# Three of a streaming kernel's loads split in two halves, one from each of two issuing queues

## The chip, the cores and the metric

The kernel runs on one core of a Trainium2 chip. A core has engines that run side by side: here ScalarE (ACT) takes exponentials (busy 124.1 us of a span of 162.2 us in the kernel before), VectorE (DVE) adds up rows (72.9 us), and SyncE (SP) issues the loads; ScalarE issues the final store, and after the change some loads too. The bytes themselves are moved by 16 DMA engines that both issuers share. A load is issued when an engine puts it on its queue. It has landed when its semaphore (a counter) has been raised for the last time: the traces show 16 raises for each load. Load 4, for instance, brings chunk 4 of the input. The metric is the device time of one execution in microseconds, lower is better. Each kernel was run several times, always in rounds beside the kernel before on the same chip.

## The reference

```python
# x: 32 x 512 x 1024, float32
x_max = np.max(x, axis=-1, keepdims=True)
return x_max.squeeze(-1) + np.log(np.sum(np.exp(x - x_max), axis=-1))
```

That is 16,384 rows of 1,024 numbers, 67.1 MB in, 64 KB out. The values come from a normal distribution, so the kernel leaves the maximum out and computes `log(sum(exp(x)))`.

## The kernel before

Each of the 128 partitions holds 128 rows of the input. They are loaded in 17 chunks into a ring of 51 row slots. A "row" below means one row for each of the 128 partitions, 512 KB.

```python
CHUNKS = [          # (rows, rows whose sum VectorE takes)
    (4, 1), (15, 11), (16, 10), (16, 15), (16, 0), (14, 0), (12, 9), (9, 5), (7, 5), (5, 4),
    (4, 3), (3, 0), (2, 2), (2, 2), (1, 0), (1, 0), (1, 0),
]
RING_ROWS = 51
...
    def load(i):
        (s, row), r = place[i], CHUNKS[i][0]
        act_wait = max(a for a, _ in busy[s : s + r])
        dve_wait = max(d for _, d in busy[s : s + r])
        if dve_wait:
            nc.sync.wait_ge(dve_done, dve_wait)
        if act_wait:
            nc.sync.wait_ge(act_done, act_wait)
        for engine, lo, hi in FIRST_PARTS if i == 0 else [("sync", 0, P)]:
            getattr(nc, engine).dma_start(
                out=ring[lo:hi, s : s + r], in_=x_v[lo:hi, row : row + r]
            ).then_inc(landed[i], 16)
...
    for i, (r, n_dve) in enumerate(CHUNKS):
        if i:
            load(i)
        ...
        nc.scalar.wait_ge(landed[i], 16 * (len(FIRST_PARTS) if i == 0 else 1))
        if n_dve:
            nc.scalar.activation(                       # one exponential over n_dve rows
                out=ring[:, s : s + n_dve], in_=ring[:, s : s + n_dve], func=Exp
            ).then_inc(act_done, 1)
            ...
            nc.vector.reduce_sum(out=sums[:, row : row + n_dve], ...)
        for j in range(n_dve, r):                       # the other rows: ScalarE sums as well
            nc.scalar.activation(..., func=Exp, accum_out=sums[:, row + j : row + j + 1])
    ...
    # take the logarithms, store the result from ScalarE
```

Chunks 0 to 3 fill the ring (4 + 15 + 16 + 16 = 51 rows), so loads 0 to 3 wait for nothing. Load 4 writes over slots of chunks 0 and 1 and waits for chunk 1's sums on VectorE; load 5 waits for those of chunk 2, loads 6 and 7 for those of chunk 3. All loads go out on SyncE's queue, the first as the first instruction of the program.

The softmax here doesn't subtract the row's maximum and nothing guards it: scores larger than these inputs give would overflow.

Of the kernel before, what the change touches and what calls it, by code (L numbers as in the profile page):

```python
# [1 line left out]

# [4 lines left out]



CHUNKS = [  # L10
# [4 lines that stand above are left out]

LN_AT = 5

FIRST_PARTS = [("sync", 0, 128)]


@with_exitstack
def kernel(
    ctx: ExitStack,
    tc: tile.TileContext,
    x: bass.AP,
    axis: bass.AP,
    out: bass.AP,
):
    nc = tc.nc
    P = nc.NUM_PARTITIONS  # L30

    assert axis in (-1, len(x.shape) - 1), f"only last-axis reduction supported, got {axis}"

    x_flat = x.flatten_outer_dims()
    N, D = x_flat.shape
    assert N % P == 0
    NB = N // P
    assert sum(r for r, _ in CHUNKS) == NB

    fp32 = mybir.dt.float32  # L40
    Exp = mybir.ActivationFunctionType.Exp
    Ln = mybir.ActivationFunctionType.Ln
    AX = mybir.AxisListType.X

    x_v = x_flat.rearrange("(p t) d -> p t d", p=P)
    out_v = bass.AP(tensor=out.tensor, offset=out.offset, ap=[[NB, P], [1, NB]])

    ring = nc.alloc_sbuf_tensor("ring", [P, RING_ROWS, D], fp32).ap()
    sums = nc.alloc_sbuf_tensor("sums", [P, NB], fp32).ap()
    res = nc.alloc_sbuf_tensor("res", [P, NB], fp32).ap()  # L50

    landed = [tc.alloc_semaphore(f"landed{i}") for i in range(len(CHUNKS))]
    act_done = tc.alloc_semaphore("act_done")
    dve_done = tc.alloc_semaphore("dve_done")
    stored = tc.alloc_semaphore("stored")


    hook = nc.pop_inst_callback()
    symbolic, nc._always_lower_symbolic_ap = nc._always_lower_symbolic_ap, False


    place = []
    row = slot = 0
    for r, _ in CHUNKS:
        if slot + r > RING_ROWS:
            slot = 0
        place.append((slot, row))
        slot += r
        row += r



    busy = [(0, 0)] * RING_ROWS
    acts = dves = 0
# [6 lines that stand above are left out]
            nc.sync.wait_ge(dve_done, dve_wait)  # L81
        if act_wait:
            nc.sync.wait_ge(act_done, act_wait)
        for engine, lo, hi in FIRST_PARTS if i == 0 else [("sync", 0, P)]:
            getattr(nc, engine).dma_start(
                out=ring[lo:hi, s : s + r], in_=x_v[lo:hi, row : row + r]
            ).then_inc(landed[i], 16)

    def take_logs(lo, hi, dve_wait, act_wait):
        nonlocal acts  # L90
        nc.scalar.wait_ge(act_done, act_wait)
        nc.scalar.wait_ge(dve_done, dve_wait)
        nc.scalar.activation(out=res[:, lo:hi], in_=sums[:, lo:hi], func=Ln).then_inc(  # L93
            act_done, 1
        )
        acts += 1

    body = nc.main_func.blocks[-1]
    assert not body.instructions
    load(0)  # L100
    n_early = len(body.instructions)

    nc.scalar.preload_act_table_set("natural_log_exp_and_others")  # L103

    logged = 0
    done_before = [(0, 0)]
    for i, (r, n_dve) in enumerate(CHUNKS):
        if i:
            load(i)
        s, row = place[i]  # L110
        if i == LN_AT:
            logged = row
            take_logs(0, logged, *done_before[i])
        nc.scalar.wait_ge(landed[i], 16 * (len(FIRST_PARTS) if i == 0 else 1))
        if n_dve:
            nc.scalar.activation(  # L116
                out=ring[:, s : s + n_dve], in_=ring[:, s : s + n_dve], func=Exp
            ).then_inc(act_done, 1)
            acts += 1
            nc.vector.wait_ge(act_done, acts)  # L120
            nc.vector.reduce_sum(  # L121
                out=sums[:, row : row + n_dve], in_=ring[:, s : s + n_dve], axis=AX
            ).then_inc(dve_done, 1)
            dves += 1
            for j in range(n_dve):
                busy[s + j] = (0, dves)
        for j in range(n_dve, r):
            nc.scalar.activation(  # L128
                out=ring[:, s + j],
                in_=ring[:, s + j],  # L130
                func=Exp,
                accum_out=sums[:, row + j : row + j + 1],
            ).then_inc(act_done, 1)
            acts += 1
            busy[s + j] = (acts, 0)
        done_before.append((dves, acts))

    take_logs(logged, NB, dves, acts)
    nc.scalar.wait_ge(act_done, acts)
    nc.scalar.dma_start(out=out_v, in_=res).then_inc(stored, 16)  # L140
    nc.gpsimd.wait_ge(stored, 16)



    first = nc.main_func.blocks[0]
    head, work = first.instructions, body.instructions
    end = next(k for k, i in enumerate(head) if i.opcode == "UnconditionalBranch")
    head, tail = head[:end], head[end:]
    for ins in work[:n_early]:
        at = next(  # L150
            k for k, i in enumerate(head) if i.engine == ins.engine and i.opcode == "Drain"
        )
        head.insert(at, ins)
    first.instructions = head + work[n_early:] + tail
    body.instructions = []

    nc._always_lower_symbolic_ap = symbolic
    nc.push_inst_callback(hook)


# [1 line left out]
_INS = ['x', 'axis']  # L162
_OUTS = [((32, 512), 'float32')]

_NUMBERS = {'axis': -1}


# [26 lines left out]
```

## Time and profile before

| | before |
|---|---|
| time, median of the first 3 runs | 164.13 us (164.01 to 164.53) |
| span of the profiled run | 162.2 us |
| ACT busy, DVE busy | 124.1 us, 72.9 us |
| bytes read, mean rate | 67.11 MB, 414 GB/s over the span |
| last load landed | 158.08 us |

The first view is the table of stretches: for each stretch of time its length, then the busy time of DVE, ACT and POOL, the clock granted to TensorE (not used here), the mean busy share of the 16 DMA engines, and the GB/s. In brackets is the number of instructions. The stretches are cut at the moments when a chunk's work starts.

```profile
0.00:7.40 7.40, 0.00 (x0) 1.28 (x1) 0.20 (x4) 1.00 1.02 416
7.40:25.60 18.20, 1.22 (x1) 4.17 (x7) 0.00 (x0) 1.00 1.01 436
25.60:45.00 19.40, 9.76 (x1) 13.77 (x10) 0.00 (x0) 1.00 1.00 432
45.00:64.30 19.30, 12.68 (x2) 14.95 (x13) 0.00 (x0) 1.00 1.00 435
64.30:83.70 19.40, 6.57 (x2) 14.05 (x4) 0.00 (x0) 1.00 0.98 426
83.70:100.60 16.90, 9.85 (x1) 16.87 (x33) 0.00 (x0) 1.00 0.99 427
100.60:158.10 57.50, 32.03 (x7) 57.50 (x68) 0.00 (x0) 1.00 0.97 415
158.10:162.20 4.10, 0.77 (x1) 1.48 (x5) 0.00 (x0) 1.00 0.06 16
```

Read the second figure from the right, the DMA share: it is 0.97 to 1.02 in every stretch up to 158.1 us. From the first packet, at 1.08 us, the engines that move the bytes are practically never idle: the trace's own packet records show 16 packets in flight at nearly every moment (exactly 16 in 94% of the moments from 2.5 to 157 us, 16.05 on average), as many as there are engines. Shares a little over 1 arise because a packet is booked whole to the stretch in which it starts. Then read ACT: in the first five stretches it has idle time (14.05 of 19.40 us busy before 83.7), from 83.7 us on it has none (57.50 of 57.50).

The second view is the timeline, here only the lines with which each chunk starts on ACT: start, duration, instruction, and in brackets how long ACT had been idle and what ended it.

```profile
7.42 1.06 ACT L116 ACTIVATE ring<-ring 128x1024 f32<-128x1024 f32 x1 [5.37 <-DMA ring<-in_x_dram]
25.62 9.59 ACT L116 ACTIVATE ring<-ring 128x11264 f32<-128x11264 f32 x1 [14.02 <-DMA ring<-in_x_dram]
44.98 8.74 ACT L116 ACTIVATE ring<-ring 128x10240 f32<-128x10240 f32 x1 [5.62 <-DMA ring<-in_x_dram]
64.36 13.00 ACT L116 ACTIVATE ring<-ring 128x15360 f32<-128x15360 f32 x1 [4.42 <-DMA ring<-in_x_dram]
83.69 1.06 ACT L128 ACTIVATE ring<-ring 128x1024 f32<-128x1024 f32 x1 [5.29 <-DMA ring<-in_x_dram]
```

Each of the first five chunks starts when its load lands. The spacing of 19.4 us between chunks of 16 rows is 1.21 us a row, which is what the DMA engines need: the packet records show one packet for each partition's piece of a load, 65,536 bytes in 2.42 us, and 16 engines at that pace make 433 GB/s.

The trace's issue records tell the third thing: SyncE issued loads 0 to 3 at 0.00, 0.78, 1.16 and 1.95 us, each taking 0.33 to 0.74 us. Load 0 is not through until about 7 us. So issue time was hidden before the change.

### The profile page before, as it was taken

How to read it: one execution, taken by the hardware profiler on the slowest of the kernel's cores; microseconds unless marked ns; L12 is line 12 of the kernel's file. 1: busy time of each engine (PE TensorE's matmuls, PEld its weight loads, DVE VectorE, ACT ScalarE, POOL GpSimd, SP SyncE). 2: the span in 40 equal slices, each digit the busy share in tenths (PEclk: the TensorE clock that was granted, in tenths of full speed). 3: DMA queues.
4: the chain of work that ended last, by engine and by line, in shares of the span. 5: the costliest groups of instructions: out<-in, count | busy, mean ns of one | idle time of the engine just before them, and what ended most of it. 6: DMA issues, size and time to landing. Idle time of an engine off the chain costs nothing.

```text
span 162.2 us, 213 instructions
## 1 busy us (share of the span) xinstructions
DVE 72.9 (45%) x11; ACT 124.1 (76%) x136; POOL 0.2 (0%) x4
## 2 busy tenths in 40 slices
DVE  0030000039960799000999900000006999799591
ACT  3180006997099971999339999999999999999993
POOL 0000000000000000000000000000000000000000
DMA  6999899969969959969988999999999999999970
GB/s 263 497 485 470 349 394 517 485 291 517 485 291 517 517 259 517 517 275 501 517 368 370 424 424 432 461 497 388 436 427 399 431 400 439 420 424 414 415 318 16
DMA packets 2593, 67.18 MB, mean 414 GB/s; under 512 B 288, under 2 KB 416, under 8 KB 800
## 3 DMA queue, kind: packets, MB, share of 16 engines
q1 hardware_dynamic: 2448, 67.11, 96.4%
q10 hardware_dynamic: 144, 0.07, 0.1%
q14 instruction: 1, 0.01, 0.0%
HBM read 67.11 MB, written 0.07 MB: 414 GB/s over the span
## 4 chain that ended last, share of the span: by engine, by line
ACT 52%; DMA 38%; DVE 7%; issue 1%
DMA ring<-in_x_dram 38%; ACT ring L128 30%; ACT ring L116 22%; DVE sums L121 7%; ACT res L93 0%
## 5 line engine op out<-in xcount | busy, mean ns | idle before, releaser
L121 DVE TENSOR_REDUCE sums<-ring 128x5 f32<-128x5120 f32 (+8 forms) x11 | 72.9, 6648 | 86.0 <-ACT ring L116 85.9
L116 ACT ACTIVATE ring<-ring 128x5120 f32<-128x5120 f32 (+8 forms) x11 | 59.3, 5394 | 29.4 <-DMA ring<-in_x_dram 29.4
L128 ACT ACTIVATE ring<-ring 128x1024 f32<-128x1024 f32 x61 | 63.4, 1041 | 5.3 <-DMA ring<-in_x_dram 5.3
L128 ACT ACTIVATION_READ_ACCUMULATOR ring<-ring 128x1 f32 x61 | 11.4, 187 | 0.0
L103 ACT ACT_TABLE_LOAD x1 | 1.3, 1283 | 0.8 <-PEq L175 0.8
L93 ACT ACTIVATE res<-sums 128x67 f32<-128x67 f32 (+1 forms) x2 | 0.5, 256 | 0.1
L175 POOL MEMSET const-bfloat16-1.0<- 128x1 bf16 x1 | 0.1, 101 | 0.0
L175 POOL MEMSET const-uint8-127<- 128x1 uint8 x1 | 0.1, 101 | 0.0
L175 POOL MEMSET const-float32-0.0<- 128x1 f32 x1 | 0.1, 98 | 0.2 <-issue 0.2
L175 POOL MEMSET const-float32-1.0<- 128x1 f32 x1 | 0.1, 98 | 0.0
## 6 DMA issues: line engine op xcount, KB each, us to landing
ring<-in_x_dram SPq DMA_DIRECT2D x1, 7680.0 KB, 24.8
ring<-in_x_dram SPq DMA_DIRECT2D x1, 7168.0 KB, 36.1
ring<-in_x_dram SPq DMA_DIRECT2D x1, 6144.0 KB, 21.6
ring<-in_x_dram SPq DMA_DIRECT2D x1, 4608.0 KB, 32.1
ring<-in_x_dram SPq DMA_DIRECT2D x2, 2048.0 KB, 26.3
ring<-in_x_dram SPq DMA_DIRECT2D x1, 3584.0 KB, 40.2
ring<-in_x_dram SPq DMA_DIRECT2D x1, 2560.0 KB, 44.4
ring<-in_x_dram SPq DMA_DIRECT2D x2, 1024.0 KB, 46.0
```

Source lines behind the costliest of these rows:

```text
L93: nc.scalar.activation(out=res[:, lo:hi], in_=sums[:, lo:hi], func=Ln).then_inc(act_done, 1)
L103: nc.scalar.preload_act_table_set("natural_log_exp_and_others")
L116: nc.scalar.activation(out=ring[:, s : s + n_dve], in_=ring[:, s : s + n_dve], func=Exp).then_inc(act_done, 1)
L121: nc.vector.reduce_sum(out=sums[:, row : row + n_dve], in_=ring[:, s : s + n_dve], axis=AX).then_inc(dve_done, 1)
L128: nc.scalar.activation(out=ring[:, s + j], in_=ring[:, s + j], func=Exp, accum_out=sums[:, row + j : row + j + 1],).then_inc(act_done, 1)
L175: nc = _bacc.Bacc("TRN2", target_bir_lowering=False, num_devices=1)
```

## The change

The intent is to put the first big loads on two issuing queues at once: loads 1, 2 and 3 are cut in two halves by rows, the first half issued by SyncE, the second by ScalarE, which is idle then (for 5.37 us before its first exponential). ScalarE's three issues stand after its table load and before its first exponential.

```diff
-FIRST_PARTS = [("sync", 0, 128)]
+SHARED = (1, 2, 3)
...
-        for engine, lo, hi in FIRST_PARTS if i == 0 else [("sync", 0, P)]:
-            getattr(nc, engine).dma_start(
-                out=ring[lo:hi, s : s + r], in_=x_v[lo:hi, row : row + r]
+        half = r // 2 if i in SHARED else r
+        nc.sync.dma_start(
+            out=ring[:, s : s + half], in_=x_v[:, row : row + half]
+        ).then_inc(landed[i], 16)
+        if half < r:
+            nc.scalar.dma_start(
+                out=ring[:, s + half : s + r], in_=x_v[:, row + half : row + r]
             ).then_inc(landed[i], 16)
...
+    for i in SHARED:
+        load(i)
...
-        if i:
+        if i and i not in SHARED:
             load(i)
...
-        nc.scalar.wait_ge(landed[i], 16 * (len(FIRST_PARTS) if i == 0 else 1))
+        nc.scalar.wait_ge(landed[i], 32 if i in SHARED else 16)
```

## The prediction

> **What bounds it now.** The table of stretches shows a DMA share of 0.97 to 1.02 in every stretch from 0 to 158.1 us (415 to 436 GB/s), against 0.06 in the last 4.1 us. Queue q1 alone takes 96.4% of 16 engines' span. In the trace's packet records 16 packets are in flight at nearly every moment: each row of 65,536 B takes 2.42 us, one of 61,440 B 2.27 us, one of 16,384 B 0.61 us, the next starting as one ends. The load stream is the floor: about 67.1 MB at 430 GB/s, plus 1.1 us before the first packet, about 1.2 us of slow first packets (0.95 to 1.36 us instead of 0.61), and 4 us of tail. ACT is the second bound: it waits for landings before 83.7 us (at 7.4, 25.6, 45.0, 64.4, 83.7), then is busy 57.50 of 57.50 us to the end, each chunk ending just as the next lands.
>
> **What the change does.** The same bytes, in 20 loads instead of 17. Removed: nothing on the DMA engines; SyncE had issued its first four loads by 2.4 us, 4 us before the first of them ended, so issue time was hidden already. Added: 24 more packets per engine. From 0.611 us for 16 KB and 2.42 us for 64 KB the fixed part of a packet is about 8 ns, so about 0.2 us in all. Three issues on ACT (0.3 to 0.75 us each, as on SyncE) fall into ACT's idle 5.37 us before its first exponential: free.
>
> **What moves.** [...] No part of this trace has two load queues at once, so the order below is an estimate. ACT's halves arrive at about 2 us, while load 0 still has some six packets per engine to go; these will alternate with 32 KB packets (1.2 us): load 0 lands at about 13 instead of 7.4. When SyncE's half of load 1 is through, ACT's queue is already most of the way through load 2's half: 25 rows have gone instead of 19, at 1.21 us a row: load 1 lands at about 33 (25.6 before), load 2 at about 52 (45.0), load 3 unchanged at 64.4.
>
> **Critical path.** Following the durations: chunk 1's sums end at 54 (47.1 before), so load 4 is issued at 54, still before the queue runs dry at 64. Chunk 2's sums end at 72, load 5 is issued then, before 82. ACT does chunk 2 until 67, chunk 3 until 81, before load 4 lands at 83.7; loads 6 and 7 go out at about 96.4 (93.6 before), before load 5's last packets at 98 to 100. All of the delay is absorbed, with about 2 us left at the tightest places. From 83.7 us on everything is as before, later by 0.2 us.
>
> **Prediction.** 164.3 us, 163.7 to 165.4. Chances: faster by over 2% 0.02, within 2% 0.92, slower by over 2% 0.06.
>
> **What would show it.** Landings of loads 0, 1, 2 later by 6 to 7 us, of loads 3 and 4 unchanged; DMA share still 1.0 from 1 to 158 us; ACT's first wait about 11 us instead of 5.4; ACT without idle after 84.
>
> **What would make it wrong.** A cost of switching between queues[...]. A landing order worse than estimated, so that ACT still has work at 83.7 or load 6 comes after the queue has run dry: each microsecond over then adds one. Faster only if two queues raise the engines' rate, or the slow first packets shrink.

The forecast's sum came to 164.1 us of the kernel before and 0.2 us for 24 more packets an engine, 164.3 us. That the two queues alternate by packet was the assumption at that point, and the landings in "What moves" are an estimate that rests on it; the packet records below show the alternation.

## The result

The changed kernel took 164.37 us (median of 4 runs, 164.19 to 164.70), the kernel before in the same comparison 164.09. The ratio is 1.0013, with a 95% interval of 0.9994 to 1.0033: the same. Ratios here and below are the mean time of one kernel's fast runs over that of the other's of the same rounds, so not quite the ratio of the medians.

The table of stretches of the changed kernel, with the same cuts:

```profile
0.00:7.40 7.40, 0.00 (x0) 1.28 (x1) 0.20 (x4) 1.00 0.90 354
7.40:25.60 18.20, 1.22 (x1) 4.17 (x7) 0.00 (x0) 1.00 1.01 434
25.60:45.00 19.40, 4.81 (x1) 13.74 (x9) 0.00 (x0) 1.00 1.00 431
45.00:64.30 19.30, 12.61 (x2) 14.30 (x12) 0.00 (x0) 1.00 1.07 462
64.30:83.70 19.40, 11.10 (x2) 14.60 (x5) 0.00 (x0) 1.00 0.98 426
83.70:100.60 16.90, 10.35 (x1) 16.64 (x32) 0.00 (x0) 1.00 0.99 427
100.60:158.10 57.50, 31.80 (x7) 57.47 (x68) 0.00 (x0) 1.00 0.97 415
```

The DMA share is full again, and the rates are the same. (The 0.90 of the first stretch and the 1.07 of the fourth come from packets booked whole to the stretch in which they start; the records show the engines taking one packet after the other in both.) The queues' lines of the page, packets, MB, and share of 16 engines' span, show where the halves went: q1 is SyncE's queue, q10 ScalarE's.

```profile
q1 hardware_dynamic: 2448, 54.53, 78.6%
q10 hardware_dynamic: 576, 12.65, 18.1%
```

Together 96.7%; before, q1 alone had 96.4%. And the starts of the chunks on ACT, from the timeline:

```profile
12.34 1.06 ACT L122 ACTIVATE ring<-ring 128x1024 f32<-128x1024 f32 x1 [10.28 <-DMA ring<-in_x_dram]
30.57 9.59 ACT L122 ACTIVATE ring<-ring 128x11264 f32<-128x11264 f32 x1 [14.05 <-DMA ring<-in_x_dram]
50.00 8.74 ACT L122 ACTIVATE ring<-ring 128x10240 f32<-128x10240 f32 x1 [5.68 <-DMA ring<-in_x_dram]
64.87 12.99 ACT L122 ACTIVATE ring<-ring 128x15360 f32<-128x15360 f32 x1
83.96 1.06 ACT L134 ACTIVATE ring<-ring 128x1024 f32<-128x1024 f32 x1 [5.06 <-DMA ring<-in_x_dram]
```

Chunks 0, 1 and 2 start 4.9 to 5.0 us later than before. Chunk 3 starts 0.5 us later and needs no wait at all (no bracket), and chunk 4 starts 0.27 us later. So the change moved three landings by 5 us, and nothing of that is left at 84 us. Two questions follow: why did they move, and why did it cost nothing?

### The profile page after: what moved, and what is told of

It reads as the page before. It is cut to its first block, busy times and chain, and to the rows that moved or that the text cites. A ratio compares the mean times of both kernels' runs of the same rounds, so it can differ in the third digit from the quotient of the medians.

```text
span 162.4 us, 216 instructions
## 1 busy us (share of the span) xinstructions
DVE 72.9 (45%) x11; ACT 123.9 (76%) x136; POOL 0.2 (0%) x4
## 4 chain that ended last, share of the span: by engine, by line
ACT 52%; DMA 38%; DVE 7%; issue 1%
DMA ring<-in_x_dram 38%; ACT ring L134 30%; ACT ring L122 22%; DVE sums L127 7%; ACT res L97 0%; ACT L107 0%
```

## The experiments

The table collects the landing of each load (when the last part of its semaphore count arrived), ScalarE's first issue and the first packet on ScalarE's queue (on the earliest of the 16 engines), all from the traces' records, in us from the span's start, and the times.

| kernel | first issue, first packet | load 0 | 1 | 2 | 3 | 4 | last | median time | ratio (95%) |
|---|---|---|---|---|---|---|---|---|---|
| before | none | 7.4 | 25.6 | 45.0 | 64.3 | 83.7 | 158.1 | 164.1 | 1 |
| the change | 0.81, 4.60 | 12.3 | 30.6 | 50.0 | 64.6 | 83.9 | 158.3 | 164.37 | 1.0013 (0.9994 to 1.0033) |
| e1 halves, one queue | none | 7.6 | 25.8 | 45.2 | 64.7 | 84.0 | 158.8 | 164.46 | 1.0024 (1.0011 to 1.0038) |
| e2 load 1 only | 0.80, 4.56 | 12.2 | 25.8 | 45.1 | 64.7 | 84.1 | 158.6 | 164.41 | 1.0013 (0.9996 to 1.0031) |
| e3 ACT after load 0 | 7.50, 11.34 | 7.5 | 30.5 | 50.1 | 74.3 | 84.0 | 164.0 | 169.71 | 1.0341 (1.0325 to 1.0356) |
| e4 ACT order 2, 1, 3 | 0.81, 4.54 | 12.3 | 40.3 | 50.0 | 64.5 | 85.7 | 160.1 | 166.03 | 1.0122 (1.0092 to 1.0152) |
| e5 ACT order 3, 1, 2 | 0.80, 4.66 | 12.4 | 40.6 | 60.0 | 64.8 | 85.8 | 164.4 | 170.19 | 1.0349 (1.0330 to 1.0367) |
| e6 ACT order 3, 2, 1 | 0.81, 4.54 | 12.3 | 59.6 | 49.9 | 64.5 | 103.4 | 179.1 | 185.28 | 1.1272 (1.1249 to 1.1294) |
| e7 half of load 4 | none | 7.5 | 25.9 | 45.3 | 64.6 | 74.3 | 154.1 | 160.02 | 0.9732 (0.9716 to 0.9748) |
| e8 half of load 5 | none | 7.6 | 25.7 | 45.1 | 64.4 | 83.8 | 153.9 | 164.02 | 0.9979 (0.9959 to 0.9999) |
| e9 load 0 in two parts | 1.28, 4.98 | 14.3 | 32.6 | 52.0 | 64.5 | 83.8 | 158.4 | one look, 164.33 | |
| e10 table after issue | 0.78, 4.79 | 12.3 | 30.5 | 50.0 | 64.5 | 83.9 | 158.7 | one look, 164.61 | |
| e11 ACT half first | 0.12, 2.81 | 16.2 | 34.4 | 54.0 | 64.9 | 84.2 | 160.2 | 166.20 | 1.0109 (1.0073 to 1.0145) |

My theory: (a) the DMA engines carry bytes at the same rate whoever issues them (432.5 GB/s from 2.5 to 64 us before, 431.6 with the change, from the packet records), so two queues can only change the order in which bytes land; (b) with two queues each engine takes packets from them in turn, so parts of later loads overtake parts of earlier ones; (c) what lands later is absorbed as long as ScalarE is through with chunk 3 when load 4 lands, and as long as each load is issued before the engines run out of work. Rivals: two queues do gain or cost something at the engines and it is offset elsewhere; or a later landing always costs a part of itself.

### Halving without the second queue

```diff
-            nc.scalar.dma_start(
+            nc.sync.dma_start(
                 out=ring[:, s + half : s + r], in_=x_v[:, row + half : row + r]
```

> The same halves, all six issued from SyncE in order. Theory A (the DMA engines are the floor; halving costs only the fixed part of 24 more packets per engine, and the 5 us later landings come from the second queue): landings of loads 0, 1, 2 back at 7.4, 25.6 and 45.0 us, load 4 at 83.9; time 164.3, as the change. Theory B (switching between queues costs something, or two queues gain something): the time differs from the change's by over 0.3 us.

The landings of loads 0 to 4 went back to within 0.4 us of before, and the time was 164.46 us, a ratio of 1.0024 in five rounds. The change's ratio, 1.0013, lies within reach of that. So the 5 us later landings come from the second queue, not from the halves. An extra 0.2 to 0.6 us (the interval of the ratio) comes with the halves already, and no cost or gain of alternating between queues is seen beside it; one under about 0.3 us could not be seen in these times. Theory A holds.

### Only load 1 shared

```diff
-SHARED = (1, 2, 3)
+SHARED = (1,)
```

(loads 2 and 3 whole, from SyncE, in their old places)

> Only load 1 is shared, loads 2 and 3 are whole from SyncE. Theory A (load 1 is late because ScalarE's queue goes on to load 2's half, and gets every second packet, while SyncE still carries load 1): load 0 lands at 12.3 us as in the change, load 1 at 25.7, load 2 at 45.1, time 164.2. Rival (load 1 is late because ScalarE's half starts late, at 4.6 us, or because two queues are slower): load 1 at about 30 us again.

Load 0 landed at 12.2 us as in the change, but load 1 at 25.8, only 0.2 us after its time of before. Both loads' bytes were there to be moved in both kernels; what differs is that ScalarE's queue had nothing behind load 1's half. In the change, ScalarE's queue went on with load 2's half, every second packet, while SyncE's queue still carried load 1.

The packet records of the change show the turns. Written out for one engine, around the end of load 0 (start, duration in us, queue, bytes):

```
 9.44  0.611  SyncE    16384   last packet of load 0 on this engine
10.04  1.213  ScalarE  32768   load 1, second half
11.26  0.009  SyncE    4       load 0's completion mark
11.26  1.213  ScalarE  32768   load 1, second half
12.47  1.062  SyncE    28672   load 1, first half
13.53  1.213  ScalarE  32768   load 1, second half
```

(The records do not name the engine; these six follow one another end to start.) In these records the queues alternate packet by packet although the packets differ in size, and the 4-byte mark that adds to the semaphore takes a turn of its own: load 0's data were complete at 10.05 us on this engine, its mark came one 32 KB packet later, and after the mark the turn went back to ScalarE's queue. The counts over all engines agree: from 5 to 10 us 43 packets of 16 KB started on SyncE's queue and 40 of 32 KB on ScalarE's, from 12.5 to 30 us 139 on each, marks included (28 KB on SyncE's queue, 32 KB on ScalarE's). The data of load 0 ended at 10.05 to 10.71 us on the 16 engines, its 16 marks at 11.26 to 11.98, and the semaphore was raised at 11.66 to 12.32. A packet here is one partition's whole piece of a load, up to 64 KB.

### ScalarE issues after load 0 has landed

```diff
     for i in SHARED:
-        load(i)
+        load(i, later=True)                 # SyncE's halves only
...
         nc.scalar.wait_ge(landed[i], 32 if i in SHARED else 16)
+        if i == 0:
+            for j in SHARED:
+                act_half(j)                 # ScalarE's halves
```

> ScalarE issues its three halves after load 0 has landed, at 7.4 us. Load 0 lands at 7.4, chunk 0 starts about 2 us later. If ScalarE's packets enter about 1 us after the issue (8.4 us): load 1 at 26.8, load 2 at 46.2, load 3 at 66.9, time 164.3. If they wait for some four packets of SyncE's that the engines have taken already (4 x 1.06 us, first packet at about 12 us): load 1 at 31 to 32, load 2 at 51, and load 3 at 72 to 77, because load 4, issued at about 51 to 53 us, now gets every second packet while ScalarE's queue still carries load 3; ScalarE then has no idle time left before load 4's chunk and the time is 166 to 171.

Load 0 landed at 7.5 us again, as load 0 is then alone. But ScalarE's first packet came at 11.34, 3.8 us after the issue, by which time SyncE's queue was well into load 1. The second branch of the expectation came true, with loads 1 and 2 up to 1 us earlier than it said: load 1 at 30.5, load 2 at 50.1, load 3 at 74.3, time 169.71 us. Load 3 is now 10 us late, since SyncE's load 4, issued at 52 us, takes every second turn, as in the records above, while ScalarE's queue still has load 3's half. The critical chain shows what that did:

```profile
74.34 13.01 ACT ring L130
87.35 0.02 issue
87.37 16.16 DVE sums L135
103.54 0.02 issue
103.55 17.57 DMA ring<-in_x_dram
```

Chunk 3's exponentials start at 74.34 instead of 64.36, its sums end 10 us later, and load 6 (issued at 103.55) waits for them. In the records the last packets of load 5 end at 100.8 and the first of load 6 start at 104.5: 3.7 us in which all engines stand idle. This run shows (b) and (c) together: one later landing that passes the slack costs time.

### The same halves in another order on ScalarE's queue

Three runs keep everything of the change, queues, packets and bytes, and only alter the order in which ScalarE issues its three halves.

```diff
+    for i in (2, 1, 3):        # e4;   (3, 1, 2) in e5;   (3, 2, 1) in e6
+        act_half(i)
```

> ScalarE issues the halves of loads 2, 1, 3 in this order; bytes, packets and queues as in the change. Theory A (the delay is absorbed as long as load 4 is issued before the queue runs dry at 64 us and ScalarE has finished chunk 3 before 83.8): load 1 lands at 40.2, load 2 at 49.9, chunk 1's sums end at 61.8 and load 4 goes out then; ScalarE ends chunk 3 at 83.0, loads 6 and 7 go out at 98.2: all slack used up, yet time 164.3 to 164.7. Rival (each microsecond of later landings costs a part of itself at the end): 15 us later than before must show as over 1 us.

The landings of loads 1 and 2, at 40.25 and 49.96 us, came to within 0.1 us of what was expected, and chunk 1's sums ended at 61.8, so load 4 was issued at 61.81. But the time was 166.03, not 164.3 to 164.7: this expectation was wrong by 1.5 us. The critical chain shows where:

```profile
49.90 11.90 DVE sums L134
61.79 0.02 issue
61.81 23.88 DMA ring<-in_x_dram
85.69 0.02 issue
```

Load 4 landed at 85.69 instead of 83.94. In the packet records, all engines are through with load 3 by 64.13 us. 14 of them start load 4 between 63.38 and 64.41 us, most as they end load 3, but two only at 65.12 and 65.29, and the first packets take 2.66 us on average and up to 3.31, instead of 2.42. The load lands with its slowest engine. I had reckoned about 1.1 us from issue to first packet, which is what the first engine shows for load 0; the last of the 16 started load 0 at 1.97 us. On engines that are at work the last one took 65.29 - 61.81 = 3.5 us. So the limit in (c) is tighter than I had it: a lead of 1.6 us, from load 4's issue to the first engine's end of load 3, was too little.

> ScalarE issues the halves of loads 3, 1, 2 in this order. Theory A (absorbed up to a limit, then one for one): load 1 at 40.2 us, load 2 at 59.6, ScalarE ends chunk 3 at 88.6 instead of 78.3, loads 6 and 7 go out at 104 us, after the queue has run dry at 100: DMA idle for some 5 us, time 168.9, and 1 to 2 us more (170 to 171), since the run with the order 2, 1, 3 showed that a load issued less than about 3 us before the queue runs dry leaves engines idle and makes their first packets slow. Rival (only the number of queues counts, not the order in them): 164.3.

Measured 170.19 us, as expected with that correction. (The "about 3 us" in this expectation, and in that of e11, is an estimate from e4, where a lead of 1.6 us was too little and the last engine began 3.5 us after the issue; no run shows a limit at 3 us.) Load 1 landed at 40.6, load 2 at 60.0, chunk 3's sums ended at 104.1, and loads 6 and 7 went out at 104.07 and 104.49. The table of stretches has the hole; DMA share and GB/s are the last two figures:

```profile
83.70:100.60 16.90, 12.71 (x1) 16.90 (x26) 0.00 (x0) 1.00 0.98 425
100.60:104.60 4.00, 3.44 (x1) 4.00 (x9) 0.00 (x0) 1.00 0.00 0
```

> ScalarE issues the halves of loads 3, 2, 1: load 1's half comes last. Theory A: load 1 lands at 59.6 us, its sums end at 81, so load 4 goes out at 81 and the DMA engines stand idle from 64 to about 83: time 183 to 185. Same bytes, packets and queues as in the change. Rival: 164.3.

Measured 185.28 us, a ratio of 1.127, 0.3 us above the range expected. After the pause the first packets of load 4 took 3.07 us on average instead of 2.42. The page's 40 slices of the span (4.58 us each, busy shares in tenths) show the engines empty for some four slices:

```profile
DMA  7999999999999700038999999997999999999960
GB/s 286 458 415 436 437 429 428 436 451 451 415 408 444 343 0 0 0 129 329 458 458 458 401 402 401 401 504 343 515 389 394 445 432 423 412 428 419 415 259 14
```

Load 1 landed at 59.6, its sums ended at 81.2, load 4 went out at 81.19, long after the queue had run dry at about 64. With the same instructions and the same two queues the time thus ranges from 164.4 to 185.3 us, by order alone. That rules out the rival that only the number of queues counts, and in the change itself the rival that any delay costs a part of itself.

### When does ScalarE's queue get its first turn?

In the change ScalarE's packets start 3.8 us after the issue, when SyncE's queue has had five packets an engine. Three runs ask why. (The four packets of theory P, below, are an estimate from the same trace: 1.1 us from issue to first packet, as for load 0, and four packets of 0.61 us make 3.5 us.)

e9 issues load 0 as two loads of 2 rows:

```diff
+        if i == 0:
+            for j in (0, 2):
+                nc.sync.dma_start(
+                    out=ring[:, j : j + 2], in_=x_v[:, j : j + 2]
+                ).then_inc(landed[0], 16)
+            return
```

> The change, with load 0 issued as two loads of 2 rows from SyncE, so that its packets are 8 KB (0.31 us) instead of 16 KB (0.61 us). Theory P (ScalarE's first packets wait behind some four packets of SyncE's queue that each engine has taken already): they start at about 3.2 us instead of 4.6, and load 0, with more turns to take, lands at about 23 us. Rival F (a fixed 3.8 us from ScalarE's issue to its first packet): they start at 4.6 us again, load 0 lands at 15 to 17.

The first packet came at 4.98 us, 3.70 after the issue (which itself was 0.47 us later than in the change), although each engine by then had taken ten or more of SyncE's small packets. That speaks against theory P and for a roughly constant time. Load 0 landed at 14.3, a little earlier than the 15 to 17 of F and far from the 23 of P.

e10 moves ScalarE's table load behind its issues:

> The change, with ScalarE's table load after its three issues instead of before them. If the table load (1.28 us on ScalarE) holds back ScalarE's packets, they start about 1.3 us earlier than 4.6 us and load 0 lands later by up to two turns; if not, they start 3.7 us after the issue as before, and nothing changes: 164.3.

First packet at 4.79 us, 4.0 after the issue: no earlier, and the landings of loads 0 to 4 are those of the change to within 0.1 us. The table load is not the reason (e3, where ScalarE issues at 7.5 us with no table load near, said so already).

e11 issues ScalarE's half of load 1 as its first instruction, with load 0:

```diff
     load(0)
+    act_half(1)
     n_early = len(body.instructions)
```

> The change, with ScalarE's half of load 1 issued as its very first instruction, at the same moment as load 0, when the DMA engines are idle. Theory I (an issue to idle engines gives its first packet after about 1.1 us, as load 0's does; 3.7 us passed only because the engines were busy): ScalarE's packets start at 1.0 to 1.7 us and alternate from the first; load 0 lands at about 17 us, load 1 at 35.3, load 2 at 54.7; loads 6 and 7 go out at 99.1, under 3 us before the queue runs dry at 100, so 1 to 2 us are lost, as in the order 2, 1, 3: time 165.3 to 166.5. Theory F (3.7 us on ScalarE's queue always): packets from 3.7 us, load 0 lands at 13.4, load 1 at 31.7, time 164.3. If two queues from the first moment shrink the slow first packets (0.95 to 1.36 us instead of 0.61), load 3 lands before 64.3.

The issue was at 0.12 us and the first packet at 2.81, 2.7 us later, when each engine had had two packets of load 0. Neither theory I (1.1 us) nor theory F (3.7) has it. Load 0 landed at 16.2, load 1 at 34.4. The time, 166.20 us, is what was expected of a late load 6: it went out at 98.05 us, 1.9 us before the first engine ran dry. Its packets started within half a microsecond of the end of load 5's, but were slow: one took 3.70 us instead of 1.82, and load 6 landed 2.0 us later than in the change (117.4 instead of 115.4). The first packets of load 0 were no quicker than before (0.84 to 1.73 us, against 0.61 to 1.36), so two queues from the first moment do not shorten the start. What is known is then: 1.1 us from the first issue to the first packet with idle engines, 2.7 us where the engines become busy meanwhile, 3.7 to 4.0 us on ScalarE's queue with busy engines, for packets of 8, 16 and 28 KB on the other queue. ScalarE's queue is not slow by itself: the final store, issued on it when the engines are idle, has its first packet 0.87 us after the issue in the kernel before, where it is the first use of that queue, and 0.86 us in the change. Nor are busy engines enough: on SyncE's queue the first engine began load 4 in e4 1.57 us after the issue. Why it takes 3.7 us and more stays open.

The traces also bound the lead that an issue needs, counted to the moment when the first engine ends the load before it. With 3.7 us (load 6 in e9) and 3.9 us (load 5 in e5) no engine paused and the packets ran at their usual pace. With 1.4 to 1.9 us (load 4 in e4 and e5, load 6 in e4 and e11) some engines paused, or their first packets were slow. The limit is not sharp, for load 6 in e6, with 1.75 us, had first packets of 1.85 us on average instead of 1.82.

### What is the limit, the loads or ScalarE?

Two runs take bytes away from the kernel before. The rows that are not loaded are computed all the same, on stale data with a scale of 0; the result is wrong, the instructions are the same.

```diff
+            n = 8 if i == 4 else r            # e7;   7 if i == 5 in e8
             getattr(nc, engine).dma_start(
-                out=ring[lo:hi, s : s + r], in_=x_v[lo:hi, row : row + r]
+                out=ring[lo:hi, s : s + n], in_=x_v[lo:hi, row : row + n]
...
                 func=Exp,
+                scale=0.0 if i == 4 and j >= 8 else 1.0,
```

> The kernel before, but load 4 brings 8 of its 16 rows (the others are computed on stale rows with a scale of 0, a wrong result on purpose; the instructions of ScalarE and VectorE are the same). Theory A (before 83.7 us the load stream is the limit; what is saved there counts until ScalarE's idle 5.3 us before chunk 4 are used up): load 4 lands at 74.0 us instead of 83.7, chunk 4 starts at 78.4 when ScalarE is through with chunk 3, time 158.8; up to 1.8 us more where load 6, which cannot be issued before 93.6, lands after ScalarE wants it (109.7 us): 158.6 to 160.6. Rival (the loads are not the limit there): 164. If the loads alone were the limit everywhere, the 9.7 us saved in bytes would show more fully than that, less the engines' idle time before load 6 (some 4 us).

Load 4 landed at 74.3 us and the time fell to 160.02, ratio 0.973. Of the 9.4 us that load 4 landed earlier, about 4.4 arrived at the end. The waits in the timeline account for it: ACT's 5.3 us of idle time before chunk 4 are gone. But load 6 has to wait for chunk 3's sums and went out at 93.87 us, as before, when the engines had been empty since 90.9 us at the latest; it landed at 111.22 and made ACT wait 1.09 us, which leaves 4.2:

```profile
111.24 7.88 ACT L117 ACTIVATE ring<-ring 128x9216 f32<-128x9216 f32 x1 [1.09 <-DMA ring<-in_x_dram]
```

> The kernel before, but load 5 brings 7 of its 14 rows (the other 7 are computed on stale rows with a scale of 0, so the result is wrong on purpose; ScalarE's and VectorE's instructions are the same). Theory A (from 83.7 us on ScalarE is as much the limit as the DMA engines): ScalarE is busy without a gap, so the time falls by under 0.6 us, to 163.5 to 164.1, although the last load lands 3 to 5 us earlier. Rival (the DMA engines alone are the limit to the end): the time falls with the landing, by about 5 us, to 159.

Load 5 landed at 92.6 us instead of 100.7 and the last load at 153.9 instead of 158.1, yet the time was 164.02 us against 164.57 in the same rounds (ratio 0.998). The table of stretches shows why:

```profile
100.60:158.10 57.50, 32.03 (x7) 57.50 (x68) 0.00 (x0) 1.00 0.91 388
153.00:158.10 5.10, 3.72 (x2) 5.10 (x6) 0.00 (x0) 1.00 0.01 5
```

From 153 to 158 us the DMA engines have nothing left to do, and ACT is busy throughout. So before 83.7 us the loads are the limit; from there on ScalarE is just as much one, and bytes saved there bring next to nothing (0.2%).

## Why the prediction was right

The prediction was 164.3 us, within 2%; the result is 164.37.

- *"The load stream is the floor", ScalarE "the second bound"*: right. A stream of packets end to end carried 432.5 GB/s before and 431.6 with the change (2.5 to 64 us); e7 shows that bytes saved before 83.7 us shorten the time, e8 that after it ScalarE alone would hold the time.
- *Nothing removed, since issue time was hidden*: right: with SyncE done issuing at 2.4 us and the engines full until 64 us, there was nothing to save.
- *About 0.2 us for 24 more packets per engine*: chunk 4 started 0.27 us later, and e1, with the halves but without the second queue, measured a ratio of 1.0024, about 0.4 us. The 0.27 us alone proves nothing: e7 and e8 do the same as the kernel before up to load 3, and it landed at 64.63 and 64.42 us there against 64.34. The size is right to within what these runs resolve; that all of it is the fixed part of packets was argued, not shown separately.
- *The two queues alternate by packet, and loads 0 to 2 land later*: right, with e2 and the packet records. The size was off: predicted 13, 33 and 52 us, measured 12.3, 30.6 and 50.0, so 5 us later rather than "6 to 7". The term that was mis-sized is ScalarE's first packet: *"ScalarE's halves arrive at about 2 us"* was 4.60 us. By then five packets of load 0 had gone on each engine instead of two.
- *All of the delay is absorbed*: right. Load 4 was issued at 52.1 us (54 predicted), load 5 at 69.6 (72), load 6 at 94.1 (96.4); ACT was through with chunk 3 in time for load 4 and idle 5.06 us before it.
- *"about 2 us left at the tightest places"*: off in size, and here there was luck, for two errors pulled against each other. The landings came 2 us earlier than estimated, which left ACT 5 us. But I had taken 1.1 us as the lead that an issue needs, and e4 and e11 show that 1.6 to 1.9 us are too little once the engines are busy, and that up to 3.5 us can pass before the last engine starts. In the change load 6 had 99.6 - 94.1 = 5.5 us, which was enough. Issued at the predicted 96.4 us it would have had 3.2, between the leads that cost time and those that did not; no run shows whether that is enough.
- *The slow first packets*, "0.95 to 1.36 us": misread. All 16 first packets of load 0 before took 0.61 to 1.36 us, 0.92 on average (0.77 to 1.62 us and 1.10 in the change). Nothing in the sum depends on it, as both kernels start the same way, and e11 shows that a second queue does not help there.
- *A cost of switching between queues* was named as what could make the prediction wrong. e1 against the change shows none (164.46 and 164.37 us): a cost of some us would have stood out, about 0.3 us would not.

## What to carry to other kernels

Before splitting loads over issuing queues, look whether the DMA engines ever stand idle: where their share was 1.0 already, as here, a second queue brought no bandwidth (164.37 us beside 164.09) and only interleaved the loads, so that the one needed first landed later (load 0 at 12.3 us instead of 7.4). If two queues are used, count packets by turns, not by bytes (16 and 28 KB packets took turns one for one with 32 KB packets here): what the second queue carried for later overtook what the first still held, and the order within ScalarE's queue decided (164 to 185 us with the same bytes). And leave an issue its lead: by these runs a load that waits for a buffer should go out some 4 us before the engines run out of work (an estimate: 3.7 us was enough in e9, 1.6 to 1.9 us were not in e4 and e11), more than the 1.1 to 2.0 us in which the 16 engines begin from idle.
